# Two groups of four column tiles in the seven-product form in the second pair of each part of the down projection

## The chip, the cores and the metric

The kernel runs on one core of a Trainium2 chip. The metric is the device time of one execution in microseconds (us), the median of several runs. Five engines matter: PE (TensorE) with its weight loads (PEld), DVE (VectorE), ACT (ScalarE), POOL (GpSimd) and SP (SyncE, which here only issues transfers).

## The reference

Two decoder layers on 256 rows of 2048 channels, in fp32. Each layer has a token mixer, a SwiGLU feed-forward part and a gated per-layer input. The change is in the feed-forward part:

```python
hf = rmsnorm(x, norm_ffn_g[i])
gate, up = jnp.split(hf @ w_gate_up[i], 2, axis=-1)   # 2048 -> 2 x 5632
x = x + (jax.nn.silu(gate) * up) @ w_down[i]          # 5632 -> 2048

hp = rmsnorm(x, norm_ple_g[i])
x = x + jax.nn.sigmoid(hp @ w_ple_gate[i]) * (p[i] @ w_ple_proj[i])
```

## The kernel before

**A product in three matmuls.** Every fp32 operand is held as a high part (rounded to the type fp32r, which TensorE multiplies) and a low part (what the rounding left). A product is xh*wh + xh*wl + xl*wh, three matmuls accumulated in PSUM (L184, L185, L186). The weights come from HBM as raw tiles of 128x1024 (512 KB), issued on SP's queue (`fetch`). `split` makes the two parts of a raw tile: a copy on ACT gives `wh` (L143), a subtraction on DVE gives `wl` (L144). There are 8 buffers for raw tiles, 5 each for `wh` and `wl`, and 28 of 128x1024 (`pair`) for operands and results. PSUM has two 128x1024 tiles (`mm`) and four 128x512 tiles (`ms`).

**Two column tiles at once.** Nearly all of the projections go through `fast_chunks`, which computes two column tiles of 512 of the output together. The K dimension is cut into groups of 512 (four column tiles of the operand). A *plain* group costs, for both output tiles, four splits and 48 matmuls (four plain pieces of one split and 12 matmuls each, from the function `go`). A *seven-product* group does the same by Winograd's form of Strassen's algorithm: each of the 2x2 blocks of x and of the weights enters through sums, and seven block products stand in place of eight, which is seven splits and 42 matmuls. Three of the seven weight blocks are sums of raw tiles made on DVE (two additions at L269, a subtraction at L270) and one is made by a transfer on POOL's queue that adds a raw tile of w1 onto one of w2 in SBUF (L274). Products p1, q5, q6, q7 accumulate over all groups in the four `ms` tiles, the others straight into the halves of the two `mm` tiles.

The order within `fast_chunks` is written out: for each seven-product group p1, c21 and one plain piece, then c11, another plain piece where enough are left (more than two per plain group), then q7, q6, q5 and c12. After the last group come the evictions of the `ms` tiles (a copy on ACT, four 128x512 operations on DVE) mixed with plain pieces. The first output tile ends with `add(u1, u1, c1())`, which is handed to `first`, the second with `sub(u2, c2(), u2)`, which is returned. There must be plain pieces for this: `left` holds two per plain group for each of the two output tiles.

**The operand of a seven-product group.** Class `Fast` takes the transposed tiles (`take`, L349), makes four sums of 128x256 on DVE (`make`, L358), and the high and low parts of all eight blocks (L367 on ACT, L368 on DVE). A plain operand is made by `halves` (L317 on ACT, L318 on DVE). Both run as a "turn": a closure in a queue that the next plain pieces call.

**The feed-forward part.** The 5632 hidden channels are 11 chunks of 512, in three parts of 3, 4 and 4 chunks (`FFN_PARTS`). Per part, the gate/up stages of its chunks run first: each is one `fast_chunks` over K = 2048 (four groups) whose two output tiles are gate and up. They use one or two seven-product groups in turn (`FAST = (2, 1)` with `FAST[c % 2]`): chunk 2, the last of part 0, uses two. The result is multiplied with the gate (L912), and its transposes (L330) and its operand are queued as a turn of the next stage. Then the down projection of the part runs as two *pairs* of output tiles, n = 0 (tiles 0 and 1) and n = 2 (tiles 2 and 3), over the part's 3 or 4 groups. Its first group, chunk c0, is in the seven-product form, the others are plain. Each output tile is added to x by `residual` (L873), a DVE operation of 128x1024. In the last part the norm of the next stage follows each of these additions: squares on ACT and, as a turn, transposes of x and their halves.

After the second pair of part 0 comes the gate/up stage of chunk 3 (one seven-product group), after that of part 1 the one of chunk 7 (one such group), after that of part 2 the gate of the per-layer input.

Of the kernel before, what the change touches and what calls it, by code (L numbers as in the profile page):

```python
# [47 lines left out]
def trunk(ctx, tc, xT, xR, pT, wI, wF, wC, wA, wOut, wGU, wD, wPG, wPP, vec, bF, gF, out):  # L48
# [15 lines left out]
    def pair(dtype=F32):  # L64
        return pairs.tile([P, 2, 512], dtype, tag="pair", name=f"pair{next(uid)}")

    def tmp():
        return tmps.tile([P, 512], F32, tag="tmp", name=f"tmp{next(uid)}")
# [104 lines left out]
    class Sum:  # L173
        def __init__(self, n, bank):
            self.n, self.left, self.bank = n, n, bank
# [34 lines left out]
    def await_x(xs, ks):  # L210
        while not all(k in xs for k in ks):
            assert turns or tasks
            run()


    def chunk(groups, xs, hook=None):
        n = sum(len(ks) for _, ks in groups)
        if n == 2:
            sums = [Sum(n, once(bank_ms)) for _ in range(2)]
        else:  # L220
            t, *sums = sums_of_blocks(n)
        for src, ks in groups:
            if hook is not None:
                parts = fetch_first(src, hook)
                hook = None
            else:
                parts = [split(fetch(src[:, o * 512 : (o + 2) * 512])) for o in range(0, len(ks), 2)]
            await_x(xs, ks)
            for j, p in enumerate(parts):
                plain(sums, xs, ks[2 * j], p)  # L230
            run()
            fill(CONV)
        return t() if n > 2 else [b.t for b in sums]
# [76 lines left out]
    def by_four(w, n=N4):  # L310
        return [(w[g], range(4 * g, 4 * g + 4)) for g in range(n)]


    def halves(o, src, scale=None):
        hi, lo = o[..., :S], o[..., S:]
        if scale is None:
            act.activation(hi, src, AF.Copy)  # L317
            dve.tensor_tensor(lo, src, hi.bitcast(F32), op=ALU.subtract)  # L318
        else:
            act.activation(hi, src, AF.Copy, scale=scale)  # L320
            dve.scalar_tensor_tensor(lo, src, scale, hi.bitcast(F32), op0=ALU.mult, op1=ALU.subtract)
# [11 lines left out]
    def by_blocks(o):  # L333

        return (lambda b: o[:, b * P : (b + 1) * P]), (lambda b: o[:, S + b * P : S + (b + 1) * P])
# [3 lines left out]
    class Fast:  # L339


        def __init__(self):
            self.f = [pair().rearrange("p a (n k s) -> p (a n) k s", n=2, k=2) for _ in range(2)]

        def take(self, half, pt, gains=None):
            src = pt.rearrange("p k (b s) -> p b k s", b=2)
            to = self.f[0][:, 2 * half : 2 * half + 2]
            if gains is None:
                act.activation(to, src, AF.Copy)  # L349
            else:  # L350
                for kk in range(2):
                    act.activation(to[:, :, kk, :], src[:, :, kk, :], AF.Copy, scale=gains[kk])
            if half == 1:
                self.make()
# [36 lines left out]
    def operand(xs, k0, src, fast=None):  # L391
        for half, pt in turned(src):
            if fast is not None:
                fast.take(half, pt)
                continue
            o = pair(F32R)
            halves(o, pt)
            for kk in range(2):
                xs[k0 + 2 * half + kk] = by_blocks(o[:, kk, :])
        if fast is not None:  # L400
            xs.update(zip(range(k0, k0 + 4), fast.column_tiles()))
# [45 lines left out]
    def advance(norm, n):  # L447

        norm.squares(n)
        turns.append(lambda: norm.turn(n))  # L450
        if n == N4 - 1:
            norm.finish()
# [51 lines left out]
    def hook():  # L504
        load_x(0, 2, 4)
        take(0)
# [9 lines left out]
    def rest(q):  # L516
        def go():
            take(q)
            load_x(q + 1) if q < 3 else None
            turns.append(rest(q + 1) if q < 3 else lambda: late(0))  # L520
        return go
# [15 lines left out]
    for i in range(L):  # L537
# [333 lines left out]
        def residual(n, acc):  # L871
            xc = xt[:, :, n * 512 : (n + 1) * 512]
            dve.tensor_tensor(xc, xc, acc, op=ALU.add)  # L873

        norm = Norm(g_ffn, fast=max(FAST))
        def onto_x(norm, n):
            def go(y):
                residual(n, y)
                if norm is not None:
                    advance(norm, n)  # L880
            return go
# [8 lines left out]
        c0 = 0  # L890
        for part, nch in enumerate(FFN_PARTS):
            hid = {}
            fast_hid = Fast()
            for c in range(c0, c0 + nch):
                w1, w2 = wGU[i, 2 * c], wGU[i, 2 * c + 1]
                o = pair() if c == 0 else None

                def gate(g):
                    nonlocal o
                    if o is None:  # L900
                        o = g
                    for b in range(2):
                        act.activation(o[:, b, :], g[:, b, :], AF.Silu, scale=norm.r(b))

                if c == 0:
                    gate(chunk(by_four(w1), norm.xs))
                    up = chunk(by_four(w2), norm.xs)
                else:
                    nf = FAST[c % len(FAST)]
                    up = fast_chunks(norm.fast[:nf], w1, w2, norm.xs, range(4 * nf, KD, 4), gate)  # L910
                for b in range(2):
                    dve.scalar_tensor_tensor(  # L912
                        o[:, b, :], up[:, b, :], norm.r(b), o[:, b, :], op0=ALU.mult, op1=ALU.mult
                    )
                turns.append(
                    lambda c=c, o=o, hid=hid, fast=fast_hid if c == c0 else None:
                    operand(hid, 4 * c, lambda b: o[:, b, :], fast)
                )
            for n in range(0, N4, 2):
                await_x(hid, (4 * c0,))  # L920
                on = after if part == len(FFN_PARTS) - 1 else None
                onto_x(on, n + 1)(
                    fast_chunks(
                        [fast_hid], wD[i, n][c0 : c0 + nch], wD[i, n + 1][c0 : c0 + nch], hid,
                        range(4 * c0 + 4, 4 * c0 + 4 * nch, 4), onto_x(on, n),
                    )
                )
            c0 += nch
            if part == len(FFN_PARTS) - 2:
                pin = tmp().rearrange("p (k s) -> p k s", k=2)  # L930
                nc.sync.dma_start(pin, pT[i])
                po = pair(F32R)
                halves(po, pin)
                ps = {k: by_blocks(po[:, k, :]) for k in range(2)}
# [119 lines left out]
```

## Time and profile before

| What | us |
| --- | --- |
| median of 3 runs | 2826.44 |
| lowest and highest run | 2826.43, 2826.75 |
| the profiled execution | 2827.59 |
| its span | 2825.9 |
| PE busy | 2803.7 |
| PE weight loads busy | 2318.0 |
| DVE busy | 2345.7 |
| ACT busy | 1581.5 |
| POOL busy | 60.0 |

PE's matmuls are pipelined: each is shown as about 0.39 us, but one starts every 0.23 us, and a stretch of such rows without a bracket behind them is one in which PE does not stop. The mean granted clock of TensorE over the span is 0.997 of full speed.

The stages that the change touches, in layer 0 of the profiled execution, in us from the span's start: the second pair of part 0 from 772.0 to 803.2, of part 1 from 1015.0 to 1057.2, of part 2 from 1269.9 to 1313.8; in layer 1 from 2174.8 to 2206.0, 2417.8 to 2460.0 and 2672.7 to 2716.4. The second chunk's operand of part 0 is made during the gate/up stage of chunk 2, from 697.2 to 739.0.

### The profile page before, as it was taken

The page shows a single profiled execution, that of the slowest core. Times are in us where ns is not written, and L with a number is a line of the kernel's source. Part 1 is how long each engine was busy: PE and PEld are TensorE (multiplying, and loading weights), DVE is VectorE, ACT ScalarE, POOL GpSimd, SP SyncE. Part 2 cuts the span into 40 slices and gives each one's busy share as a digit, 9 for nine tenths or more (in the row PEclk, how much of TensorE's full clock was granted, in tenths as well). Part 3 has the DMA queues.
Part 4 walks back from the last instruction along what each step waited for, and adds up shares of the span by engine and source line. Part 5 has one row for each costly group of instructions (what it writes and reads, how often), then busy time and mean ns, then how long its engine had stood idle before and what let it go on. Part 6 is the DMA issues. An engine that isn't in the chain of part 4 may idle for free.

```text
span 2825.9 us, 34767 instructions
## 1 busy us (share of the span) xinstructions
PE 2803.7 (99%) x12684; PEld 2318.0 (82%) x12684; DVE 2345.7 (83%) x2835; ACT 1581.5 (56%) x1912; POOL 60.0 (2%) x99
## 2 busy tenths in 40 slices
PE   9999999999999999999999999999999999999998
PEld 7888788888888888888888887888888888888886
DVE  6998877777989878888869988678689889788887
ACT  6445755565556545556644457455555465455665
POOL 0000000000000000000000000000000000000000
PEclk9999999999999999999999999999999999999999
DMA  8555466566676666666655545665656676576673
GB/s 296 183 183 187 152 215 199 192 208 192 216 224 221 203 216 217 215 216 201 214 173 189 185 165 179 209 200 180 227 188 210 220 228 221 192 231 210 204 238 123
DMA packets 158428, 573.71 MB, mean 203 GB/s; under 512 B 17840, under 2 KB 18096, under 8 KB 158000
## 3 DMA queue, kind: packets, MB, share of 16 engines
q1 hardware_dynamic: 149040, 539.50, 55.7%
q0 software_dynamic: 8352, 30.41, 5.9%
q8 instruction: 99, 1.62, 0.2%
q10 hardware_dynamic: 864, 1.57, 0.2%
q14 instruction: 73, 0.60, 0.1%
HBM read 569.32 MB, written 2.10 MB: 202 GB/s over the span
## 4 chain that ended last, share of the span: by engine, by line
PE 91%; DVE 6%; ACT 1%; issue 1%; DMA 0%; SPq 0%; POOLq 0%; POOL 0%; DVEq 0%; ACTq 0%
PE mm L184 26%; PE mm L186 26%; PE mm L185 26%; PE ms L184 4%; PE ms L185 4%; PE ms L186 4%; DVE pair L561 3%; DVE wl L144 2%; PE ms L330 2%; ACT wh L143 1%; PE ms L718 0%; DVE raw L269 0%; PE ms L747 0%; PE ms L737 0%; DMA pair<-in_xT_dram 0%
## 5 line engine op out<-in xcount | busy, mean ns | idle before, releaser
L143 ACT ACTIVATE wh<-raw 128x1024 fp32r<-128x1024 f32 x1188 | 1239.9, 1059 | 1122.4 <-PE mm L186 750.7
L144 DVE TENSOR_TENSOR wl<-raw,wh 128x1024 fp32r<-128x1024 f32 x1188 | 1434.9, 1224 | 380.8 <-ACT wh L143 375.4
L184 PE MATMUL mm<-wh,pair 128*128 128x512 f32 x3452 | 1352.9, 392 | 6.1 <-ACT wh L166 3.0
L186 PE MATMUL mm<-wh,pair 128*128 128x512 f32 x3452 | 1346.0, 390 | 0.0
L185 PE MATMUL mm<-wl,pair 128*128 128x512 f32 x3452 | 1345.7, 390 | 0.3 <-DVE wl L144 0.3
L184 PEld LDWEIGHTS mm<-wh,pair 128*128 128x128 f32 x3452 | 648.8, 188 | 139.7 <-ACT wh L166 3.2
L186 PEld LDWEIGHTS mm<-wh,pair 128*128 128x128 f32 x3452 | 648.7, 188 | 135.3
L185 PEld LDWEIGHTS mm<-wl,pair 128*128 128x128 f32 x3452 | 648.9, 188 | 133.3 <-DVE wl L144 0.7
L561 DVE SCALAR_TENSOR_TENSOR pair<-pair,vecs,pair 128x256 f32<-128x256 f32 x480 | 203.6, 492 | 0.0
L184 PE MATMUL ms<-wh,pair 128*128 128x512 f32 x496 | 193.5, 391 | 1.9 <-ACT wh L143 1.9
L186 PE MATMUL ms<-wh,pair 128*128 128x512 f32 x496 | 193.1, 389 | 0.0
L185 PE MATMUL ms<-wl,pair 128*128 128x512 f32 x496 | 193.1, 389 | 0.0
L269 DVE TENSOR_TENSOR raw<-raw,raw 128x1024 f32<-128x1024 f32 x116 | 141.8, 1222 | 1.9
L184 PEld LDWEIGHTS ms<-wh,pair 128*128 128x128 f32 x496 | 93.1, 188 | 23.6 <-ACT wh L143 3.0
L186 PEld LDWEIGHTS ms<-wh,pair 128*128 128x128 f32 x496 | 93.0, 188 | 19.4
L185 PEld LDWEIGHTS ms<-wl,pair 128*128 128x128 f32 x496 | 93.1, 188 | 18.8
L269 DVE TENSOR_TENSOR pair<-pair,ms 128x512 f32<-128x512 f32 x144 | 94.2, 683 | 0.0
L270 DVE TENSOR_TENSOR pair<-mm,pair 128x1024 f32<-128x1024 f32 (+1 forms) x49 | 59.0, 1203 | 18.9 <-PE mm L186 18.9
L270 DVE TENSOR_TENSOR raw<-raw,raw 128x1024 f32<-128x1024 f32 x58 | 71.0, 1225 | 1.9
L269 DVE TENSOR_TENSOR pair<-pair,mm 128x1024 f32<-128x1024 f32 x48 | 58.5, 1219 | 11.9 <-PE mm L186 11.9
L330 PEld LDWEIGHTS ms<-ident,pair 128*128 128x128 f32 x336 | 39.1, 140 | 5.6
L330 PE MATMUL ms<-ident,pair 128*128 128x128 f32 x336 | 43.5, 272 | 0.0
(166 smaller groups left out, 1027.8 us busy)
## 6 DMA issues: line engine op xcount, KB each, us to landing
raw<-in_wGU_dram SPq DMA_DIRECT2D x352, 512.0 KB, 4.8
raw<-in_wI_dram SPq DMA_DIRECT2D x287, 512.0 KB, 3.9
raw<-in_wD_dram SPq DMA_DIRECT2D x176, 512.0 KB, 5.4
raw<-in_wOut_dram SPq DMA_DIRECT2D x64, 512.0 KB, 4.7
raw<-in_wPG_dram SPq DMA_DIRECT2D x64, 512.0 KB, 4.9
raw<-in_wA_dram SPq DMA_DIRECT2D x32, 512.0 KB, 4.3
raw<-in_wC_dram SPq DMA_DIRECT2D x32, 512.0 KB, 5.1
raw<-in_wGU_dram POOLq DMA_DIRECT2D x30, 512.0 KB, 8.2
```

Of the source, the lines that this page charges most:

```text
L143: act.activation(h, raw, AF.Copy)
L144: dve.tensor_tensor(l, raw, h.bitcast(F32), op=ALU.subtract)
L184: pe.matmul(self.t, lhsT=xh, rhs=wh, start=start, stop=False)
L185: pe.matmul(self.t, lhsT=xh, rhs=wl, start=False, stop=False)
L186: pe.matmul(self.t, lhsT=xl, rhs=wh, start=False, stop=self.left == 0)
L269: add = lambda o, a, b: dve.tensor_tensor(o, a, b, op=ALU.add)
L270: sub = lambda o, a, b: dve.tensor_tensor(o, a, b, op=ALU.subtract)
L330: pe.transpose(pt[:, kk * S + b * P : kk * S + (b + 1) * P], src(b)[:, c : c + P], ident)
L561: dve.scalar_tensor_tensor(cv[c], u[c][:, j : j + S], w, cv[c], op0=ALU.mult, op1=ALU.add,)
```

## The change

Each part now has two `Fast` operands, for its chunks c0 and c0 + 1. The first pair (n = 0) of the down projection uses one of them as before, and reads the second chunk through the plain parts that `Fast` also holds. The second pair (n = 2) sends both through the seven-product form, and has one plain group less: one in part 0, two in parts 1 and 2. A `Fast` takes its two scratch tiles when its first transposes arrive, not when it is created. Nothing else is edited; line numbers behind L343 rise by two, and behind the second edit by two or three.

```diff
 class Fast.__init__
-            self.f = [pair().rearrange("p a (n k s) -> p (a n) k s", n=2, k=2) for _ in range(2)]
+            self.f = None
 class Fast.take
+            if half == 0:
+                self.f = [pair().rearrange("p a (n k s) -> p (a n) k s", n=2, k=2) for _ in range(2)]
 the feed-forward part
-            fast_hid = Fast()
+            fast_hid = [Fast() for _ in range(2)]
...
-                    lambda c=c, o=o, hid=hid, fast=fast_hid if c == c0 else None:
+                    lambda c=c, o=o, hid=hid, fast=fast_hid[c - c0] if c < c0 + 2 else None:
                     operand(hid, 4 * c, lambda b: o[:, b, :], fast)
...
+                nf = 1 if n == 0 else 2
                 onto_x(on, n + 1)(
                     fast_chunks(
-                        [fast_hid], wD[i, n][c0 : c0 + nch], wD[i, n + 1][c0 : c0 + nch], hid,
-                        range(4 * c0 + 4, 4 * c0 + 4 * nch, 4), onto_x(on, n),
+                        fast_hid[:nf], wD[i, n][c0 : c0 + nch], wD[i, n + 1][c0 : c0 + nch], hid,
+                        range(4 * (c0 + nf), 4 * (c0 + nch), 4), onto_x(on, n),
```

How the change moves instructions, at three places, on DVE; the names are the program's tile names with running numbers, then the size. A row with `wl` on its left is the low half of a split.

First, the middle of the second pair of part 0, layer 0. Before, from the sums of raw tiles of its only seven-product group to the first evictions of `ms` tiles:

```order
L269 TENSOR_TENSOR raw1210_6441<-raw1210_6441,raw1211_6444 128x1024
L270 TENSOR_TENSOR raw1209_6439<-raw1210_6441,raw1209_6439 128x1024
L144 TENSOR_TENSOR wl1232_6530<-raw1210_6441,wh1231_6529 128x1024
L269 TENSOR_TENSOR raw1212_6446<-raw1212_6446,raw1210_6441 128x1024
L144 TENSOR_TENSOR wl1235_6542<-raw1209_6439,wh1234_6541 128x1024
L144 TENSOR_TENSOR wl1238_6554<-raw1212_6446,wh1237_6553 128x1024
L144 TENSOR_TENSOR wl1241_6571<-raw1239_6568,wh1240_6570 128x1024
L270 TENSOR_TENSOR pair1207_6437<-pair1207_6437,ms1233_6533 128x512
```

With the change, from the first low half of the second group to the only plain piece behind that group (the last row):

```order
L144 TENSOR_TENSOR wl1246_6581<-raw1241_6571,wh1245_6580 128x1024
L144 TENSOR_TENSOR wl1248_6591<-raw1243_6576,wh1247_6590 128x1024
L144 TENSOR_TENSOR wl1251_6603<-raw1249_6600,wh1250_6602 128x1024
L144 TENSOR_TENSOR wl1253_6619<-raw1244_6578,wh1252_6618 128x1024
L144 TENSOR_TENSOR wl1255_6629<-raw1242_6573,wh1254_6628 128x1024
L269 TENSOR_TENSOR raw1242_6573<-raw1242_6573,raw1243_6576 128x1024
L270 TENSOR_TENSOR raw1241_6571<-raw1242_6573,raw1241_6571 128x1024
L144 TENSOR_TENSOR wl1257_6640<-raw1242_6573,wh1256_6639 128x1024
L269 TENSOR_TENSOR raw1244_6578<-raw1244_6578,raw1242_6573 128x1024
L144 TENSOR_TENSOR wl1259_6651<-raw1241_6571,wh1258_6650 128x1024
L144 TENSOR_TENSOR wl1261_6662<-raw1244_6578,wh1260_6661 128x1024
L144 TENSOR_TENSOR wl1264_6681<-raw1262_6678,wh1263_6680 128x1024
```

A second group with three sums of raw tiles and seven splits stands where evictions and plain pieces stood; one plain piece (the third row) lies inside the group and one behind it.

Second, the end of the same pair and the start of the gate/up stage of chunk 3. Before (the first three rows are plain pieces of the pair; raw 1261 and above belong to the next stage):

```order
L144 TENSOR_TENSOR wl1250_6627<-raw1248_6624,wh1249_6626 128x1024
L144 TENSOR_TENSOR wl1253_6645<-raw1251_6642,wh1252_6644 128x1024
L144 TENSOR_TENSOR wl1256_6663<-raw1254_6660,wh1255_6662 128x1024
L269 TENSOR_TENSOR pair1207_6437<-pair1207_6437,mm1222_6476 128x1024
L144 TENSOR_TENSOR wl1266_6694<-raw1261_6684,wh1265_6693 128x1024
L873 TENSOR_TENSOR xt_82<-xt_82,pair1207_6437 128x2x512
L144 TENSOR_TENSOR wl1269_6705<-raw1263_6689,wh1268_6704 128x1024
L144 TENSOR_TENSOR wl1273_6718<-raw1271_6715,wh1272_6717 128x1024
L144 TENSOR_TENSOR wl1276_6735<-raw1264_6691,wh1275_6734 128x1024
L270 TENSOR_TENSOR pair1208_6438<-mm1218_6463,pair1208_6438 128x1024
L144 TENSOR_TENSOR wl1279_6747<-raw1277_6744,wh1278_6746 128x1024
L873 TENSOR_TENSOR xt_82<-xt_82,pair1208_6438 128x2x512
```

With the change (the first row is the pair's last plain piece; the low half of the next stage's first product follows two rows later, its third in the last row):

```order
L144 TENSOR_TENSOR wl1264_6681<-raw1262_6678,wh1263_6680 128x1024
L270 TENSOR_TENSOR pair1209_6445<-pair1209_6445,ms1235_6541 128x512
L144 TENSOR_TENSOR wl1272_6710<-raw1267_6700,wh1271_6709 128x1024
L269 TENSOR_TENSOR pair1210_6446<-pair1209_6445,ms1232_6529 128x512
L144 TENSOR_TENSOR wl1275_6721<-raw1269_6705,wh1274_6720 128x1024
L269 TENSOR_TENSOR pair1209_6445<-pair1209_6445,ms1238_6553 128x512
L269 TENSOR_TENSOR pair1210_6446<-pair1210_6446,ms1238_6553 128x512
L269 TENSOR_TENSOR pair1209_6445<-pair1209_6445,mm1224_6484 128x1024
L270 TENSOR_TENSOR pair1210_6446<-mm1220_6471,pair1210_6446 128x1024
L875 TENSOR_TENSOR xt_82<-xt_82,pair1209_6445 128x2x512
L875 TENSOR_TENSOR xt_82<-xt_82,pair1210_6446 128x2x512
L144 TENSOR_TENSOR wl1279_6734<-raw1277_6731,wh1278_6733 128x1024
```

Before, all four evictions of `ms` lay ahead of these rows, and the second addition to x came behind the next stage's fifth low half; now the four evictions, the two operations on `mm` tiles (L269, L270) and both additions to x (L875) all lie between the pair's last low half and the third low half of the next stage.

Third, the operand of the second chunk of part 0, near the end of the gate/up stage of chunk 2. Before:

```order
L269 TENSOR_TENSOR pair1081_5835<-pair1081_5835,mm1096_5874 128x1024
L144 TENSOR_TENSOR wl1160_6190<-raw1155_6180,wh1159_6189 128x1024
L318 TENSOR_TENSOR pair1141_6110<-ms1140_6105,pair1141_6110 128x2x256
L318 TENSOR_TENSOR pair1143_6118<-ms1142_6113,pair1143_6118 128x2x256
L144 TENSOR_TENSOR wl1163_6201<-raw1157_6185,wh1162_6200 128x1024
L144 TENSOR_TENSOR wl1167_6214<-raw1165_6211,wh1166_6213 128x1024
L144 TENSOR_TENSOR wl1170_6231<-raw1158_6187,wh1169_6230 128x1024
L270 TENSOR_TENSOR pair1082_5836<-mm1092_5861,pair1082_5836 128x1024
```

With the change:

```order
L269 TENSOR_TENSOR pair1079_5833<-pair1079_5833,mm1094_5872 128x1024
L144 TENSOR_TENSOR wl1162_6198<-raw1157_6188,wh1161_6197 128x1024
L360 TENSOR_TENSOR pair1140_6109<-pair1139_6108 128x256 x2
L360 TENSOR_TENSOR pair1140_6109<-pair1140_6109,pair1139_6108 128x256
L144 TENSOR_TENSOR wl1165_6209<-raw1159_6193,wh1164_6208 128x1024
L360 TENSOR_TENSOR pair1140_6109<-pair1139_6108,pair1140_6109 128x256
L370 TENSOR_TENSOR pair1143_6122<-pair1139_6108,pair1142_6121 128x1024
L144 TENSOR_TENSOR wl1169_6222<-raw1167_6219,wh1168_6221 128x1024
L370 TENSOR_TENSOR pair1145_6126<-pair1140_6109,pair1144_6125 128x1024
L144 TENSOR_TENSOR wl1172_6239<-raw1160_6195,wh1171_6238 128x1024
L270 TENSOR_TENSOR pair1080_5834<-mm1090_5859,pair1080_5834 128x1024
```

The two halves of 128x512 read from PSUM (L318) became four sums of 128x256 (L360) and two subtractions of 128x1024 (L370), the last of them two low halves further back.

Over the whole kernel PE has 36 matmuls less, DVE 60 operations more, ACT 30 more, and POOL issues 6 accumulating transfers more; SP issues as many as before.

## The prediction

> **What bounds the kernel now.** I read the busy times first, then the chain that ended last, then tables by stage, then the timelines of PE and DVE around the changed pairs.
>
> ```profile
> PE 2803.7 (99%) x12684; PEld 2318.0 (82%) x12684; DVE 2345.7 (83%) x2835; ACT 1581.5 (56%) x1912; POOL 60.0 (2%) x99
> ...
> PE 91%; DVE 6%; ACT 1%; issue 1%; DMA 0%; SPq 0%; POOLq 0%; POOL 0%; DVEq 0%; ACTq 0%
> ```
>
> PE carries 91% of the chain, so a matmul less is time less wherever the others keep up. DVE at 83% is an average. The stages differ (core 0; columns: window in us, its length, then busy us and count of PE, PEld, DVE, ACT, POOL, granted clock, DMA share, GB/s):
>
> ```profile
> 772.00:803.20 31.20, 31.20 (x139) 25.86 (x138) 27.95 (x26) 16.09 (x16) 0.86 (x1) 1.00 0.69 217
> 803.20:845.40 42.20, 42.20 (x188) 34.91 (x187) 31.89 (x29) 21.66 (x22) 1.70 (x2) 1.00 0.71 224
> 845.40:887.10 41.70, 41.70 (x189) 34.61 (x188) 41.22 (x42) 27.43 (x29) 0.84 (x1) 1.00 0.64 206
> ...
> 1015.00:1057.20 42.20, 42.20 (x188) 34.92 (x187) 33.55 (x31) 20.73 (x21) 0.86 (x1) 1.00 0.64 211
> 1269.90:1313.80 43.90, 43.90 (x203) 36.49 (x202) 36.27 (x38) 25.95 (x36) 0.86 (x1) 1.00 0.65 215
> ...
> 2174.80:2206.00 31.20, 31.20 (x139) 25.86 (x138) 27.95 (x26) 16.08 (x16) 0.84 (x1) 1.00 0.65 217
> ```
>
> The first, fourth and fifth rows are the second pairs of parts 0, 1 and 2 in layer 0; the last is part 0's in layer 1 and repeats the first, so I cost one layer and double it. The second row is the gate/up chunk after part 0. The third row is a gate/up chunk that already sends two groups through seven products: PE never stops in it, but DVE is busy 41.22 of 41.70 us. That form runs at the edge of DVE, and the change puts it where there is less plain work to cover it.
>
> **What is saved.** PE's pace in part 0's second pair, from its first matmul to the first of the next stage, 138 matmuls on:
>
> ```profile
> 771.96 0.39 PE L184 MATMUL ms<-wh,pair 128*128 128x512 f32 x1
> ...
> 785.78 0.39 PE L185 MATMUL mm<-wl,pair 128*128 128x512 f32 x1
> ...
> 803.24 0.39 PE L184 MATMUL ms<-wh,pair 128*128 128x512 f32 x1
> ```
>
> (803.24 - 771.96) / 138 = 0.2267 us each. A plain group is 48 matmuls, a seven-product group 42; six groups change, so 36 matmuls go: 36 x 0.2267 = 8.2 us, 1.36 us at each of six places. If nothing else moved, that would be the gain.
>
> **What is added.** These rows are DVE in the two-group gate/up stage, from the low half of a split in group 1 to the first low half after the second group's evictions:
>
> ```profile
> 855.16 9.33 DVE L144 TENSOR_TENSOR wl<-raw,wh 128x1024 fp32r<-128x1024 f32 x8
> 864.53 1.23 DVE L269 TENSOR_TENSOR raw<-raw,raw 128x1024 f32<-128x1024 f32 x1
> 865.79 1.23 DVE L270 TENSOR_TENSOR raw<-raw,raw 128x1024 f32<-128x1024 f32 x1
> 866.96 1.23 DVE L144 TENSOR_TENSOR wl<-raw,wh 128x1024 fp32r<-128x1024 f32 x1
> 868.11 1.22 DVE L269 TENSOR_TENSOR raw<-raw,raw 128x1024 f32<-128x1024 f32 x1
> 869.24 4.79 DVE L144 TENSOR_TENSOR wl<-raw,wh 128x1024 fp32r<-128x1024 f32 x4
> 873.95 0.68 DVE L270 TENSOR_TENSOR pair<-pair,ms 128x512 f32<-128x512 f32 x1
> 874.54 1.22 DVE L144 TENSOR_TENSOR wl<-raw,wh 128x1024 fp32r<-128x1024 f32 x1
> 875.68 0.68 DVE L269 TENSOR_TENSOR pair<-pair,ms 128x512 f32<-128x512 f32 x1
> 876.28 1.22 DVE L144 TENSOR_TENSOR wl<-raw,wh 128x1024 fp32r<-128x1024 f32 x1
> 877.41 1.28 DVE L269 TENSOR_TENSOR pair<-pair,ms 128x512 f32<-128x512 f32 x2
> 878.61 1.22 DVE L269 TENSOR_TENSOR pair<-pair,mm 128x1024 f32<-128x1024 f32 x1
> 879.74 1.22 DVE L144 TENSOR_TENSOR wl<-raw,wh 128x1024 fp32r<-128x1024 f32 x1
> ```
>
> An operation on 128x1024 starts about 1.135 us after the one before it (876.28 to 877.41), one on 128x512 0.60 us (875.68 to 876.28). From 855.16 to 879.74 there stand 19 operations of the first size and 4 of the second, without a gap: 24.58 us.
>
> A group moved to seven products has seven splits instead of four and three sums of raw tiles: six operations more, 6 x 1.135 = 6.8 us of DVE. The second chunk's operand is now made like the first's:
>
> ```profile
> L358 DVE TENSOR_TENSOR pair<-pair,pair 128x256 f32<-128x256 f32 x2 | 0.8, 424 | 0.0
> L358 DVE TENSOR_TENSOR pair<-pair 128x256 f32<-128x256 f32 x2 | 0.8, 423 | 0.0
> L368 DVE TENSOR_TENSOR pair<-pair,pair 128x1024 fp32r<-128x1024 f32 x2 | 2.5, 1226 | 0.0
> ```
>
> About 1.4 + 2.3 us in place of two 128x512 halves (1.2), so 2.5 more. Parts 1 and 2 make it in a gate/up chunk with one seven-product group, where DVE has slack (second row, 10.3 us): zero. Part 0 makes it at the end of a two-group chunk; four plain pieces of 2.72 us follow the last product there while DVE needs 1.135 for each. I take zero; without that cover it is 2.5 us of delay.
>
> *Part 0, where the sum is decided.* DVE needs 27.95 + 6.8 = 34.8 us and PE only 31.2 - 1.4 = 29.8: 5 us short. Take the queues from the end of group 1's last product:
>
> ```profile
> 779.26 1.23 DVE L144 TENSOR_TENSOR wl<-raw,wh 128x1024 fp32r<-128x1024 f32 x1
> ...
> 781.53 3.65 DVE L144 TENSOR_TENSOR wl<-raw,wh 128x1024 fp32r<-128x1024 f32 x3
> 785.11 0.68 DVE L270 TENSOR_TENSOR pair<-pair,ms 128x512 f32<-128x512 f32 x1
> ```
>
> The second split of the row of three is that product's: its low half is ready at 784.05, PE uses it at 785.78, a lead of 1.73 us. The third starts at 783.97. In the new order the stretch from there to the low half of the next stage's third piece has 12 low halves, 3 sums, one addition and one subtraction out of the mm banks and two additions to x, 19 of 128x1024, and 4 evictions of 128x512: exactly the composition measured above, 24.58 us. So the row behind that low half can start at 783.97 + 24.58 = 808.55, and the low half itself is written at about 808.65. PE has by then issued 132 matmuls of the pair, 12 of the next stage's first two products, and one each of its third piece and its q7: 146 x 0.2267 = 33.1, at 771.96 + 33.1 = 805.05. PE waits 3.6 us. Going on with the same durations, the fourth, seventh and eighth pieces after it are within 0.1 to 0.4 us of their low halves, another 0.85 together; then plain pieces restore the lead. Stall 4.4 us against 1.36 saved: 3.0 us lost. Low end 3.2 (5 us less the 1.73 of lead); high end 6.5 (two 1.135 us operations more of delay).
>
> [...]
>
> *Part 1.* Four plain pieces follow the second group, as in the third row's stage, and DVE's 33.55 + 6.8 = 40.4 stays under PE's 40.8. Stall zero, at most one operation, 1.1 us: 1.36 saved.
>
> *Part 2.* 36.27 + 6.8 = 43.1 against 42.5: 0.5 us short, and transposes of x in the next stage wait for the last addition to x. I take 0.6, from zero (the lead covers it) to 2.3 (both additions late in full): 0.76 saved.
>
> *ACT, transfers, buffers.* ACT has three more high halves per group, 3.2 us, in stages where it is busy 16 of 31 us. Each place has one more accumulating transfer from POOL.
>
> ```profile
> raw<-in_wGU_dram POOLq DMA_DIRECT2D x30, 512.0 KB, 8.2
> raw<-in_wD_dram POOLq DMA_DIRECT2D x12, 512.0 KB, 9.8
> ...
> L143 ACT ACTIVATE wh<-raw 128x1024 fp32r<-128x1024 f32 x22 | 22.9, 1059 | 14.2 <-DVE raw L269 8.7 <-PE mm L186 3.9 <-PE ms L186 1.1
> ```
>
> In the two-group stage (last row) ACT waits for DVE's sums and for PE, not for a transfer; 8 to 10 us fit into the 15 us from group to group. Zero; uncovered, one landing would cost its 9.8 us. Taking the operand's buffers later moves no instruction of another stage: zero.
>
> **Sum.** Per layer 3.0 - 1.36 - 0.76 = +0.9; two layers +1.8 us. The profiled execution took 2827.59 us (span 2825.9 and 1.7 around it) and would take 2829.4. It lies 1.15 above the median of the runs, so the forecast is 2826.44 + 1.8 = 2828.2 us. Two tenths of a per cent, about what a measurement of this kernel tells from no change, is 5.7 us: no change that can be told.
>
> **Rivals.**
> *All of it is gained.* The third row's stage speaks for it: two such groups, no stop of PE. Against it: that stage has four plain pieces after its second group, part 0 one. 2826.44 - 8.2 = 2818.3.
> *Half the stall.* If DVE enters part 0's second group some 2 us earlier than the rows say, the stall is 2.2 and the sum -2.6: 2823.8.
> *DVE's delay spreads (slower).* DVE is the bound in part 0 and stays late: the stage after it is itself short of slack in its first group, and parts 1 and 2 pay too. With the high ends 2 x (6.5 + 1.1 + 2.3 - 4.1) = +11.6: 2838. It becomes slower than can be measured from 6.9 us of stall a layer (2 x 6.9 - 8.2 = 5.7).
> *The clock gate drops (slower).* Before the first matmuls PE idled 3 us (PE timeline, then three windows; the clock is the third number from the end):
>
> ```profile
> 8.04 0.79 PE L184 MATMUL mm<-wh,pair 128*128 128x512 f32 x1 [2.96 <-ACT wh L166]
> ...
> 4.12:7.54 3.42, 0.96 (x9) 0.77 (x7) 1.32 (x4) 1.88 (x5) 0.00 (x0) 1.00 1.06 374
> 7.54:10.95 3.41, 2.91 (x6) 2.08 (x7) 2.95 (x6) 2.70 (x5) 0.00 (x0) 0.50 0.99 345
> 10.95:14.36 3.41, 3.41 (x9) 2.64 (x9) 2.99 (x6) 3.41 (x8) 0.00 (x0) 0.50 1.02 419
> ```
>
> After a window of 3.42 us in which PE was busy 0.96 the clock was 0.50 for two windows. A stall of 3.6 us that fills such a window would cost half of 6.8 us: 3.4 each time, 2828.2 + 2 x 3.4 = 2835. [...]
>
> **Chances.** Forecast 0.60, half the stall 0.12, all gained 0.09, delay spreads 0.13, clock 0.06. The range for 8 in 10 runs from 2823.5 (leaving out the full gain) to 2833.0 (leaving out the upper ends of the last two). Faster by over 0.2%: the full gain and a little of the half stall, 0.10. Slower: most of the spread and half of the clock case with a little over, 0.15. Within: 0.75.
>
> **What would show it.** PE has 36 matmuls fewer. In the stage after part 0's second pair PE waits once for over 2 us on DVE's low half (L144) at its third piece, in both layers, and DVE has no idle time from the second group through that point. Parts 1 and 2 end 1.4 and about 0.8 us shorter without such a wait. The clock stays 1.00. The forecast is wrong if PE's wait there is under 2 us, if DVE shows gaps in that stretch, or if PE waits on L143 for a transfer.

## The result and the profile after

The median went from 2826.70 to 2832.76 us: 6.06 us slower, a ratio of 1.0019 with a 95% interval of 1.0012 to 1.0026. The forecast was 2828.2, in a range of 2823.5 to 2833.0. So the range held the time and the sign was right, but the number was 4.6 us too low. The forecast called its own time no change that can be told; the loss of 0.21% lies just beyond the 0.2% that it took for that, and the interval excludes no change. The executions of the changed kernel lie further apart (2830.8 to 2834.0) than those of the kernel before (2826.2 to 2827.6), and in two groups: seven of the 15 up to 2831.5 and eight from 2832.76 on. The median is the lowest time of the upper group; one execution more in the lower one would have made it 2831.5. Two more profiles below show where the groups come from.

The page of the changed kernel, busy times and chain that ended last:

```profile
PE 2801.3 (99%) x12648; PEld 2312.7 (82%) x12648; DVE 2398.1 (85%) x2895; ACT 1611.2 (57%) x1942; POOL 65.2 (2%) x105
...
PE 86%; DVE 10%; issue 3%; ACT 1%; DMA 0%; SPq 0%; DVEq 0%; POOLq 0%; POOL 0%; ACTq 0%
```

PE issues 36 matmuls less, as forecast. Its share of the chain fell from 91% to 86%, and DVE's rose from 6% to 10%: PE now waits for DVE at places where it did not. The shares do not say how long, since the chain, followed back from such a wait, runs on along DVE's queue: four per cent are 113 us, and the waits listed below grew by some 8 us. The table by stage says where (same columns as before; each window goes from the first matmul of a stage to the first of the next one; in order: part 0's second pair, the gate/up stage of chunk 3 behind it, then the second pairs of parts 1 and 2):

```profile
772.10:802.00 29.90, 29.90 (x134) 24.75 (x133) 29.45 (x27) 18.93 (x19) 0.84 (x1) 1.00 0.73 211
802.00:850.30 48.30, 44.88 (x187) 35.76 (x186) 37.12 (x35) 21.66 (x22) 1.70 (x2) 0.96 0.68 217
...
1019.90:1060.70 40.80, 40.80 (x181) 33.78 (x181) 40.11 (x37) 23.81 (x24) 0.86 (x1) 1.00 0.63 210
1273.40:1316.00 42.60, 42.60 (x197) 35.37 (x196) 42.02 (x44) 28.97 (x39) 0.86 (x1) 1.00 0.68 220
```

Against before, the three pairs are shorter by 1.3 (31.2 to 29.9), 1.4 (42.2 to 40.8) and 1.3 us (43.9 to 42.6), the saving of six matmuls each. The gate/up stage behind part 0 is longer by 6.1 us (42.2 to 48.3), and its granted clock is 0.96. Layer 1 repeats it (48.4). PE's waits over the whole span (columns: us in total, times, longest) name what it waits for; these three rows are new or longer:

```profile
PE mm L185 <- DVE wl L144: 5.7, 5, 2.4
...
PE mm L184 <- DVE pair L269: 1.3, 2, 0.7
...
PE mm L186 <- DVE pair L318: 1.1, 2, 0.6
```

The place itself, first on DVE (the end of the long stretch, to the low half of the third piece and those behind it), then on PE:

```profile
802.79 1.21 DVE L269 TENSOR_TENSOR pair<-pair,mm 128x1024 f32<-128x1024 f32 x1
803.92 1.21 DVE L270 TENSOR_TENSOR pair<-mm,pair 128x1024 f32<-128x1024 f32 x1
805.06 2.34 DVE L875 TENSOR_TENSOR xt<-xt,pair 128x1024 f32<-128x1024 f32 x2
807.33 4.62 DVE L144 TENSOR_TENSOR wl<-raw,wh 128x1024 fp32r<-128x1024 f32 x4
```

```profile
804.15 0.47 PE L184 MATMUL mm<-wh,pair 128*128 128x512 f32 x1 [0.64 <-DVE pair L269]
...
805.84 0.39 PE L184 MATMUL ms<-wh,pair 128*128 128x512 f32 x1
808.59 0.79 PE L185 MATMUL mm<-wl,pair 128*128 128x512 f32 x1 [2.37 <-DVE wl L144]
809.18 0.63 PE L186 MATMUL mm<-wh,pair 128*128 128x512 f32 x1
809.61 0.63 PE L184 MATMUL mm<-wh,pair 128*128 128x512 f32 x1
...
811.75 0.51 PE L186 MATMUL mm<-wh,pair 128*128 128x512 f32 x1
812.09 0.40 PE L184 MATMUL mm<-wh,pair 128*128 128x512 f32 x1
```

DVE comes to the third piece with its queue full and starts that low half at 807.33; one operation of 1.2 us later PE goes on, at 808.59. The forecast had this low half written at about 808.65. PE waits twice, not once: 0.9 us (0.8 and slower starts right behind) at the stage's second product, whose `mm` tile is free only when DVE has added it into the pair's result (L269, 802.79), and 2.5 us ahead of the third piece (starts 805.84 to 808.59, less one pace of 0.227). Together that is 3.4 us; the forecast had 3.6 in one wait.

Then comes what the forecast did not have in its sum. Behind the wait the matmuls start 0.43 us apart, not 0.23, until 812.09. The windows of that place show the granted clock (third number from the end):

```profile
805.18:808.59 3.41, 1.05 (x5) 0.53 (x3) 3.41 (x4) 0.00 (x0) 0.00 (x0) 1.00 0.00 0
808.59:812.10 3.51, 3.51 (x9) 2.79 (x10) 3.48 (x4) 0.00 (x0) 0.00 (x0) 0.52 0.51 161
```

The clock fell to a half for nearly all of 3.5 us, which costs some 1.6 us (the stage with and without the fall, below): the rival in which the clock drops came true, at half its price.

The ledger per layer, in us (a plus is time lost):

| Term | forecast | measured |
| --- | --- | --- |
| matmuls saved, 3 places | -4.1 | -4.1 |
| waits for DVE behind part 0's second pair | +4.4 | +4.6 |
| the same, by the clock that falls | 0 | 0 or +1.6 |
| part 2's shortage of DVE | +0.6 | 0 |
| part 0's second operand, in its first pair | 0 | +0.9 |
| sum | +0.9 | +1.4 or +3.0 |

Two layers with the clock falling in both give +6.0, in one of them +4.4; from 2826.7 that is 2832.7 and 2831.1 us, the two groups of times. The 4.6 is from an execution in which the clock did not fall in layer 0 (below): the stage took 46.8 us there, 42.2 before.

### The profile page after: what moved, and what is told of

Its sections match the earlier page's. It is cut to its first block, busy times and chain, and to the rows that moved or that the text cites. A ratio compares the mean times of both kernels' runs of the same rounds, so it can differ in the third digit from the quotient of the medians.

```text
span 2831.3 us, 34835 instructions
## 1 busy us (share of the span) xinstructions
PE 2801.3 (99%) x12648; PEld 2312.7 (82%) x12648; DVE 2398.1 (85%) x2895; ACT 1611.2 (57%) x1942; POOL 65.2 (2%) x105
## 4 chain that ended last, share of the span: by engine, by line
PE 86%; DVE 10%; issue 3%; ACT 1%; DMA 0%; SPq 0%; DVEq 0%; POOLq 0%; POOL 0%; ACTq 0%
PE mm L185 24%; PE mm L186 24%; PE mm L184 24%; DVE wl L144 4%; PE ms L185 4%; PE ms L186 4%; PE ms L184 4%; DVE pair L563 2%; PE ms L330 2%; ACT wh L143 1%; DVE raw L269 1%; DVE pair L269 0%; DVE pair L270 0%; PE ms L720 0%; DVE raw L270 0%
## 5 line engine op out<-in xcount | busy, mean ns | idle before, releaser
L143 ACT ACTIVATE wh<-raw 128x1024 fp32r<-128x1024 f32 x1206 | 1258.0, 1059 | 1091.4 <-PE mm L186 687.3
L184 PE MATMUL mm<-wh,pair 128*128 128x512 f32 x3392 | 1330.4, 392 | 6.9 <-ACT wh L166 2.3
L185 PE MATMUL mm<-wl,pair 128*128 128x512 f32 x3392 | 1324.2, 390 | 6.0 <-DVE wl L144 5.7
L186 PE MATMUL mm<-wh,pair 128*128 128x512 f32 x3392 | 1324.5, 390 | 1.1 <-DVE pair L318 1.1
L184 PEld LDWEIGHTS mm<-wh,pair 128*128 128x128 f32 x3392 | 638.2, 188 | 139.7 <-ACT wh L143 4.3
L185 PEld LDWEIGHTS mm<-wl,pair 128*128 128x128 f32 x3392 | 638.3, 188 | 138.8 <-DVE wl L144 8.8
L186 PEld LDWEIGHTS mm<-wh,pair 128*128 128x128 f32 x3392 | 637.7, 188 | 134.9 <-DVE pair L318 2.0
L184 PE MATMUL ms<-wh,pair 128*128 128x512 f32 x544 | 212.2, 391 | 1.9 <-ACT wh L143 1.9
L185 PE MATMUL ms<-wl,pair 128*128 128x512 f32 x544 | 211.8, 389 | 0.0
L186 PE MATMUL ms<-wh,pair 128*128 128x512 f32 x544 | 211.7, 389 | 0.0
L269 DVE TENSOR_TENSOR raw<-raw,raw 128x1024 f32<-128x1024 f32 x128 | 156.4, 1222 | 2.1
L184 PEld LDWEIGHTS ms<-wh,pair 128*128 128x128 f32 x544 | 102.1, 188 | 25.5 <-ACT wh L143 3.0
L186 PEld LDWEIGHTS ms<-wh,pair 128*128 128x128 f32 x544 | 102.1, 188 | 21.4
L185 PEld LDWEIGHTS ms<-wl,pair 128*128 128x128 f32 x544 | 102.1, 188 | 20.6
L269 DVE TENSOR_TENSOR pair<-pair,ms 128x512 f32<-128x512 f32 x144 | 93.8, 678 | 0.0
L270 DVE TENSOR_TENSOR raw<-raw,raw 128x1024 f32<-128x1024 f32 x64 | 78.4, 1225 | 2.1
L270 DVE TENSOR_TENSOR pair<-mm,pair 128x1024 f32<-128x1024 f32 (+1 forms) x49 | 58.8, 1200 | 17.0 <-PE mm L186 17.0
L269 DVE TENSOR_TENSOR pair<-pair,mm 128x1024 f32<-128x1024 f32 x48 | 58.3, 1216 | 8.5 <-PE mm L186 8.5
L370 DVE TENSOR_TENSOR pair<-pair,pair 128x1024 fp32r<-128x1024 f32 x44 | 53.2, 1217 | 0.0
L369 ACT ACTIVATE pair<-pair 128x1024 fp32r<-128x1024 f32 x44 | 46.1, 1058 | 2.4 <-DVE pair L360 1.2
```

What stands on the lines that cost most here:

```text
L143: act.activation(h, raw, AF.Copy)
L184: pe.matmul(self.t, lhsT=xh, rhs=wh, start=start, stop=False)
L185: pe.matmul(self.t, lhsT=xh, rhs=wl, start=False, stop=False)
L186: pe.matmul(self.t, lhsT=xl, rhs=wh, start=False, stop=self.left == 0)
L269: add = lambda o, a, b: dve.tensor_tensor(o, a, b, op=ALU.add)
L270: sub = lambda o, a, b: dve.tensor_tensor(o, a, b, op=ALU.subtract)
```

## The experiments

**Part 0 as before, parts 1 and 2 changed**, and the reverse. The second `Fast` and the second group are made only where the part is one of those:

```diff
-            fast_hid = [Fast() for _ in range(2)]
+            fast_hid = [Fast() for _ in range(1 if part == 0 else 2)]
...
-                nf = 1 if n == 0 else 2
+                nf = 1 if n == 0 else len(fast_hid)
```

> Parts 1 and 2 as in the change, part 0 as before. Theory A (the whole loss sits in part 0: DVE is late there, and parts 1 and 2 keep 1.36 us each): four times 1.36 us faster than before, 2826.7 - 5.4 = 2821.3 us. Rival B (the loss is spread: every second operand and every second group costs DVE time that PE waits for somewhere): no faster than before, 2826 to 2828 us.

Measured: 2821.46 us (2821.26 to 2822.42), ratio to the kernel before 0.9981 (0.9973 to 0.9990). That is 5.3 us faster, against 5.4 expected. Theory A holds and rival B falls. The stage behind part 0 is back at its old length, with no wait:

```profile
772.00:803.20 31.20, 31.20 (x139) 25.87 (x138) 27.91 (x27) 16.08 (x16) 0.86 (x1) 1.00 0.67 216
803.20:845.40 42.20, 42.20 (x187) 34.95 (x187) 31.92 (x30) 21.66 (x22) 1.70 (x2) 1.00 0.71 221
```

This version beats both kernels.

> Part 0 as in the change, parts 1 and 2 as before. Theory A: the changed kernel without the gain of four places, 2832.8 + 5.4 = 2838.2 us, with a wait of PE on DVE's low half of 2.4 us and a slower stretch of matmuls behind it in both layers. Rival B: about a third of the loss of 6 us, near 2829 us.

Measured, with the two numbers of the first line exchanged (`2 if part == 0 else 1`): 2838.1 us (2835.0 to 2839.0), ratio 1.0035 (1.0022 to 1.0049), 11.3 us slower. Theory A had 2838.2, rival B 2829 and falls. The trace has the wait of 2.5 us and the clock at a half behind it in both layers. The two halves add up: -5.3 + 11.3 = +6.0 us, the whole change +6.06. That they do so to a tenth is luck, since the five times lie in two groups as well (2835.0 and 2835.8, then 2838.1 to 2839.0). The loss is part 0's alone.

**The operands without their use**: `nf = 1` in every pair, two `Fast` in every part.

> Both operands are made in each part, and all pairs use one seven-product group as before. Theory A: 0.9 us a layer in part 0's first pair, where PE waits for the low half of chunk 2's operand because DVE is behind with the second operand of chunk 1; nothing in parts 1 and 2: 2826.7 + 1.8 = 2828.5 us. Rival B (operands cost in every part): 2826.7 + 3 x 1.8 = 2832. Rival C (the 0.9 us came from the accident of a later start): 2826.7 us.

Measured: 2828.9 us (2828.5 to 2829.9), ratio 1.0007 (0.9998 to 1.0016). The median is 2.1 us above before, and the size fits theory A, though the interval does not exclude no change. The trace shows the wait in both layers, and in part 0 only, so rivals B and C fall, but theory A's cause is wrong. The place on PE, here and, in the second fence, before the change:

```profile
755.31 0.39 PE L185 MATMUL mm<-wl,pair 128*128 128x512 f32 x1
756.27 0.50 PE L186 MATMUL mm<-wh,pair 128*128 128x512 f32 x1 [0.57 <-DVE pair L318]
```

```profile
755.72 0.50 PE L184 MATMUL mm<-wh,pair 128*128 128x512 f32 x1 [0.53 <-ACT pair L317]
756.05 0.63 PE L185 MATMUL mm<-wl,pair 128*128 128x512 f32 x2
756.51 0.40 PE L186 MATMUL mm<-wh,pair 128*128 128x512 f32 x1
```

And DVE's low halves of chunk 2's operand at that place, before the change and (second fence) in the changed kernel:

```profile
756.96 1.29 DVE L318 TENSOR_TENSOR pair<-ms,pair 128x512 fp32r<-128x512 f32 x2
```

```profile
755.56 1.28 DVE L318 TENSOR_TENSOR pair<-ms,pair 128x512 fp32r<-128x512 f32 x2
```

DVE is not behind: its low halves start at 755.56, where before they started at 756.96 (the pair started at 738.2 and 739.0, so 17.4 and 18.0 us into it). PE's order is what moved. Before the change, the L186 at 756.51 runs ahead of that low half, so it belongs to another piece. In the instruction order of PE before, eight matmuls of another plain piece stand between the first product with the new operand's high half and the first that needs its low half (weights 1186 and 1187 are that piece's, 1196 and 1197 the other's; running numbers cut to what matters):

```
L184 mm1168<-wh1186,pair1189
L185 mm1168<-wl1187,pair1189
L185 mm1164<-wl1197,pair1141
... (seven more with 1196 and 1197)
L186 mm1168<-wh1186,pair1189
```

With the second operand the order is chosen anew, L184, L185 and L186 of one piece follow each other, and PE stands before L186 until the low half is there: 0.7 us and some slower starts, 0.9 in all. Whether another order of PE would save this was not tried.

**Ten matmuls more in the wait.** In the gate/up stage behind part 0's second pair, ten products of parts of the stage's operand go onto a bank that the stage's own product q7 overwrites later (`idle` is 10 there and 0 elsewhere); the program's order puts three of them ahead of the second product and seven ahead of the third piece:

```diff
             product(c21, f(N4X), a22)
+            for _ in range(idle):
+                pe.matmul(q7.t, lhsT=f(B11)[0](0), rhs=f.h[0][:, :2].rearrange("p n k s -> p (n k s)"), start=True, stop=True)
             go()
```

> The changed kernel with ten matmuls more in each layer, 128x512 of fp32r onto a bank that the next product overwrites, ahead of the third piece of the stage after part 0's second pair; nothing reads their result. They last 10 x 0.227 = 2.3 us and fit into PE's two waits there (0.9 and 2.5 us). Theory A with the clock (PE's matmuls start 0.43 us apart for 3.5 us behind the wait, because the granted clock falls to a half after the idle stretch): the clock stays 1.00, 1.7 us a layer come back, 2832.8 - 3.4 = 2829.4 us in spite of 20 matmuls more. Rival D (the matmuls behind the wait are slow because of what DVE or the transfers do at that time): the slow stretch stays, 2832.8 us or more.

Measured: 2829.86 us (2829.5 to 2830.9), ratio to before 1.0011 (1.0003 to 1.0020): 2.9 us faster than the changed kernel, with 20 matmuls more. The place on PE and its windows:

```profile
805.46 1.77 PE L279 MATMUL ms<-pair 128*128 128x512 f32 x7
807.07 0.39 PE L184 MATMUL mm<-wh,pair 128*128 128x512 f32 x1
807.29 0.39 PE L184 MATMUL ms<-wh,pair 128*128 128x512 f32 x1
808.44 0.50 PE L185 MATMUL mm<-wl,pair 128*128 128x512 f32 x1 [0.76 <-DVE wl L144]
808.78 0.40 PE L186 MATMUL mm<-wh,pair 128*128 128x512 f32 x1
```

```profile
805.18:808.59 3.41, 2.65 (x12) 1.86 (x12) 3.41 (x4) 0.00 (x0) 0.00 (x0) 1.00 0.00 0
808.59:812.10 3.51, 3.51 (x16) 2.85 (x17) 3.48 (x4) 0.00 (x0) 0.00 (x0) 1.00 0.52 169
```

PE goes on with the low half at the same time (808.44 against 808.59), so the added matmuls cost nothing; the clock stays 1.00, in layer 1 too, and the slow stretch is gone while DVE does the same work as before beside it (3.48 us in that window in both). One trace would not be enough, since the changed kernel's own clock does not fall each time (below). The eleven times bear it out: they lie within 1.4 us, near the 2829.4 of theory A, and all but one below the lowest of the 15 of the changed kernel. Rival D falls: the slow stretch came from PE having idled. The longest gap ahead of it in the changed kernel was 2.5 us.

**One addition to x moved behind.** Both additions to x of part 0's second pair are queued as turns of the next stage. In the order that results, one of them stands behind the sixth low half of that stage and the other stays ahead of the third:

```diff
+                late = lambda m: lambda y: turns.append(lambda: residual(m, y))
+                to_x = late if part == 0 and n == 2 else lambda m: onto_x(on, m)
-                onto_x(on, n + 1)(
+                to_x(n + 1)(
```

> The changed kernel, with the two additions to x of part 0's second pair queued as turns of the next stage; on DVE one of them now stands behind the next stage's sixth low half, the other stays ahead of the third. Theory A (the wait is DVE's queue, operation by operation): the third low half comes 1.14 us earlier, PE's waits there fall from 3.4 to 2.3 us. If the clock still falls, 2832.8 - 2.3 = 2830.5 us; if a wait of 1.4 us in one piece no longer brings it down, 2832.8 - 2 x (1.14 + 1.7) = 2827.1 us. Rival E (something else than DVE's queue holds the piece, a transfer or a bank): 2832.8 us.

Measured: 2829.07 us (2828.6 to 2829.7), ratio to before 1.0007 (0.9998 to 1.0016): 3.7 us faster than the changed kernel, between the two numbers of theory A. DVE and, in the second fence, PE:

```profile
804.88 1.22 DVE L875 TENSOR_TENSOR xt<-xt,pair 128x1024 f32<-128x1024 f32 x1
806.02 4.62 DVE L144 TENSOR_TENSOR wl<-raw,wh 128x1024 fp32r<-128x1024 f32 x4
810.56 1.22 DVE L875 TENSOR_TENSOR xt<-xt,pair 128x1024 f32<-128x1024 f32 x1
```

```profile
807.29 0.50 PE L185 MATMUL mm<-wl,pair 128*128 128x512 f32 x1 [1.22 <-DVE wl L144]
807.63 0.40 PE L186 MATMUL mm<-wh,pair 128*128 128x512 f32 x1
```

The low half starts at 806.02 in place of 807.33, and PE's wait there falls from 2.5 to 1.4 us, by the length of one operation: it is DVE's queue, and rival E falls. The clock no longer fell, in either layer. What was not expected is a new wait for a high half, by PE's waits from 735 to 860:

```profile
PE mm L184 <- ACT wh L143: 0.7, 1, 0.7
```

The moved addition (810.56) stands ahead of the group's sums of raw tiles, from which such high halves are made; that it causes this wait is likely, but was not tried by itself. So 1.9 us a layer came back, not 2.8.

**Both additions on POOL**, which is idle there (0.00 us busy in the two windows of the wait):

```diff
+                by_pool = lambda m: lambda y: residual(m, y, nc.gpsimd)
+                to_x = by_pool if part == 0 and n == 2 else lambda m: onto_x(on, m)
```

> The changed kernel, with the two additions to x of part 0's second pair on POOL, which is idle there, and not on DVE. Theory A: the third low half comes 2.27 us earlier, PE's waits fall from 3.4 to about 1.1 us, the clock stays 1.00: 2832.8 - 2 x (2.27 + 1.7) = 2824.8 us. Rival F (POOL's additions slow DVE's down while they run, so little is won): 2829 us or more. Rival E (a transfer or a bank holds the piece): 2832.8 us. It stays above the kernel with part 0 left alone (2821.5 us), since the second operand's 0.9 us and the waits left cost more than the 1.36 us saved.

Measured: 2832.03 us (2831.5 to 2833.0), ratio to before 1.0017 (1.0008 to 1.0026), no more than 0.7 us under the changed kernel. Theory A missed by 7 us and rival F holds. DVE, then POOL, then PE:

```profile
805.03 2.58 DVE L144 TENSOR_TENSOR wl<-raw,wh 128x1024 fp32r<-128x1024 f32 x1
807.53 3.42 DVE L144 TENSOR_TENSOR wl<-raw,wh 128x1024 fp32r<-128x1024 f32 x1
810.87 2.35 DVE L144 TENSOR_TENSOR wl<-raw,wh 128x1024 fp32r<-128x1024 f32 x2
```

```profile
804.13 2.39 POOL L875 TENSOR_TENSOR xt<-xt,pair 128x1024 f32<-128x1024 f32 x1 [13.32 <-DVE pair L269]
806.50 3.37 POOL L875 TENSOR_TENSOR xt<-xt,pair 128x1024 f32<-128x1024 f32 x1
```

```profile
807.67 0.50 PE L185 MATMUL mm<-wl,pair 128*128 128x512 f32 x1 [1.46 <-DVE wl L144]
```

DVE starts the four low halves 2.3 us earlier, as expected, but the two that run beside POOL's additions (2.39 and 3.37 us) take 2.58 and 3.42 us, and the two behind them 2.35 together, their usual time. The four take 8.19 us, where they took 4.62. The clock stayed 1.00; the waits for slow low halves took its place: the stage is 5.7 us longer than before the change (47.9), where the changed kernel's, with the clock's fall, was 6.1 us longer. What slowed DVE's operations beside POOL's was not shown.

**The changed kernel again, for two more profiles.**

> The changed kernel once more, for its profile alone. Its times lie between 2830.8 and 2834.0 us, further apart than those of the variant with ten matmuls in the wait (2829.5 to 2830.9). Theory G: the clock does not fall in every execution. An execution near 2831 us shows the clock at 1.00 behind the wait in one layer or both, one near 2833 us shows it fall in both layers, 1.8 us each. Rival H: the clock falls in both layers whatever the time, and the times differ elsewhere.

> As the one before: a third profile of the changed kernel, with the same two expectations. Theory G: about 1.8 us between executions that differ in one fall of the clock. Rival H: no relation.

Measured: 2830.96 and 2831.44 us; the execution profiled first took 2832.97. The stage behind part 0, layer 0 and layer 1, in the profile of 2830.96:

```profile
801.60:848.40 46.80, 43.46 (x188) 34.57 (x187) 37.16 (x35) 21.45 (x22) 1.71 (x2) 1.00 0.69 221
2205.90:2254.20 48.30, 44.88 (x187) 35.76 (x186) 37.16 (x35) 22.01 (x23) 1.74 (x2) 0.96 0.68 214
```

Here the clock stayed 1.00 in layer 0 and the stage took 46.8 us; in layer 1 it fell, and the stage took 48.3. The third profile reads the same (46.8 and 48.4), the first had 48.3 and 48.4. PE's wait is the same in the layer without a fall:

```profile
808.23 0.50 PE L185 MATMUL mm<-wl,pair 128*128 128x512 f32 x1 [2.35 <-DVE wl L144]
```

So theory G holds in these three executions: 1.6 us between a layer with a fall and one without, and the two faster ones have one fall where the slower one has two. Rival H falls. Against the 42.2 us before, the stage without a fall lost 4.6 us; the forecast said 4.4.

The traces also show where the clock fell and where it did not. In the first profile of the changed kernel the granted clock changes at 9.84, 13.25, 808.56, 811.97, 2214.85, 2218.26 and 2822.42 us: from the program's start to its end, all changes lie on one grid of 3.413 us. In that of the kernel before they lie on such a grid too (7.54, 14.36 and 2816.71), and the grid lies elsewhere in each execution. These are windows of the grid at the wait, first where the clock stayed (2830.96, layer 0), then where it fell (2831.44, layer 1); those of the first profile are the two shown with its wait, to 0.04 us:

```profile
803.26:806.67 3.41, 2.09 (x8) 1.42 (x8) 3.41 (x4) 1.46 (x2) 0.00 (x0) 1.00 0.01 5
806.67:810.09 3.42, 1.86 (x8) 1.55 (x9) 3.42 (x4) 0.00 (x0) 0.00 (x0) 1.00 0.23 68
```

```profile
2210.89:2214.30 3.41, 1.37 (x6) 1.13 (x7) 3.41 (x4) 0.00 (x0) 0.00 (x0) 1.00 0.06 18
2214.30:2217.72 3.42, 3.42 (x10) 2.65 (x9) 3.35 (x4) 0.07 (x1) 0.00 (x0) 0.50 0.79 249
```

In the first, the grid cuts the same wait in two, PE is busy 2.09 and 1.86 us of the two windows, and the clock stays. In the second, PE is busy 1.37 us of one window, and the clock is 0.50 throughout the next. In all traces with two seven-product groups in part 0's second pair, every window at this place with PE busy 1.05 to 1.37 us was followed by a fall (six), and where the emptiest window had 1.70 us or more none came (eight layers). With ten matmuls more, PE is busy over 2.6 us of any 3.41 us around the wait, with one addition moved over 2.0, with both on POOL over 1.9, wherever the grid lies.

## Why the prediction was right in direction and too low

- **Saved matmuls**: right, 1.36 us at each place, and parts 1 and 2 alone give 5.3 us.
- **The stall of part 0**: right in place, cause and size. The stretch of 24.58 us taken from the two-group stage put the low half at 808.65; it was written 0.1 us earlier. Counting starts was the better choice: by the rows' durations laid end to end (19 x 1.22 + 4 x 0.68 = 25.9 us) the low half would have come 1.3 us later, and it did not. What it missed is that the same lateness shows first as a wait for an `mm` tile; the sum of both waits is what the forecast had.
- **The clock**: the step that failed. The rival had 0.06, the author's own estimate. Two waits with a few matmuls between them were enough, in four of six layers seen: wherever they fell into one window so that PE was busy no more than 1.37 of its 3.41 us. Its price was taken from the start of the program, two windows at half speed, 3.4 us; here it was one window each time, 1.6 us, and one at the program's start too in the first profile of the changed kernel (9.84 to 13.25 us). One or two falls make 1.6 to 3.2 of the 4.6 us that were missing. Which of the two the median shows is chance, with seven times in one group and eight in the other.
- **Part 0's second operand**: taken as zero, with 2.5 us of delay on DVE as the other end. It cost 0.9 us a layer, 1.8 in all, but by another way than DVE's time: a new order of PE's own matmuls took away the work that had covered the low half.
- **Part 2**: 0.6 was taken and nothing was lost. DVE is busy 42.02 of 42.60 us there, and PE does not stop. That is 1.2 us in the other direction, and it hid a part of the error.
- **Part 1, transfers, buffers**: right at zero. No wait for a transfer appears at these places, nor one for the operands' buffers.

The terms that were left out, 1.8 for the operand and 1.6 to 3.2 for the clock, with 0.4 by which the waits of both layers were longer and less the 1.2 of part 2, make +4.4 to +6.0 with the forecast's +1.8. The median moved by 6.06, the upper end. Single profiles differ by more than the sum shows: the gate/up stage of chunk 2, ahead of every place that the change touches, starts at 697.2 us before and at 696.0 to 696.5 in the three of the changed kernel. "Slower by over 0.2%", which had 0.15, is what came, by a narrow margin.

## What to carry to other kernels

A form that trades matmuls for work of another engine paid here only where plain work stood behind it (5.3 us in parts 1 and 2, a loss of 11.3 in part 0): read the margin per stage, over the stretch from the last operand in time to the first that is late, and use the form where that stretch has slack. A wait of PE cost more than its length here where the clock came down behind it, 1.6 us a fall: look how long PE is busy in the windows of 3.413 us around a stall. Those with 1.05 to 1.37 us here were followed by a fall; where the emptiest had 1.70 us or more, none came. Before an operation is moved to an idle engine, look whether it slows the busy one: beside POOL's additions two operations of DVE took 2.58 and 3.42 us in place of 1.22.

Two seven-product groups in the first pairs were not run. From the program's text, the last chunk's transposes would need an `ms` tile there while the open sums hold the four, so the order would probably have to be rewritten first.

## What the runs showed of the hardware

- The granted clock fell to a half (0.50 over one window) behind PE waits of 2.5 us (with one of 0.9 us shortly ahead) in four of six layers of the changed kernel (three profiles), and in both layers with part 0 changed alone. It did not fall behind waits of 0.9, 1.4 and 1.6 us in the experiments, two layers each. The changes of the clock lie on a grid of 3.413 us, placed anew in each execution (with an edge at 808.56 us in the first profile and at 806.67 in that of 2830.96), and each of these falls lasted one such window, so slow matmuls set in anywhere from the end of the wait to 1.4 us after it. PE was busy 1.05 to 1.37 us of the window ahead of each fall; where the emptiest window had 1.70 us or more, no fall came.
- Ten matmuls a layer that nobody reads made the kernel 2.9 us faster: the clock was 1.00 in the window from 808.59 to 812.10 where it had been 0.52.
- Two additions of 128x1024 on POOL took 2.39 and 3.37 us, and the two subtractions of the same size that DVE ran beside them took 2.58 and 3.42 us in place of 1.22. The two behind them took their usual time, 2.35 us together.
